# Sliding-window attention on one core: scores from 64-row products, the sink in the score tile, value differences

## The chip, the cores and the metric

The kernel runs on one core of a Trainium2 chip. Time is device time of that core in microseconds, from three timed runs; the profile is one further execution of the same program, taken by the hardware profiler. The core's engines are TensorE (PE, with its weight loads listed apart as PEld), VectorE (DVE), ScalarE (ACT), GpSimd (POOL) and SyncE (SP), which here only issues DMAs.

## The reference

One decoder layer on 2048 tokens of width 1024. A common input projection feeds two groups: a gated linear recurrence (HGRN2, 4 heads of 128) and causal sliding-window attention (8 query heads of 64 on 2 key/value heads, window 128, a learned sink logit per head). Their gated outputs go through an output projection, a residual and a layer norm. What the change touches is the attention:

```python
def swa_with_sinks(q, k, v, sinks):
    ...
    s = jnp.einsum('bnqhgd,bnkhd->bnhgqk', qb, kw).astype(jnp.float32) * (D ** -0.5)
    ...
    band = (j > t) & (j <= t + W)
    ...
    s = jnp.where(mask[None, :, None, None], s, -jnp.inf)
    ...
    m = jnp.maximum(jnp.max(s, axis=-1, keepdims=True), sink)
    p = jnp.exp(s - m)
    denom = jnp.sum(p, axis=-1, keepdims=True) + jnp.exp(sink - m)
    p = (p / denom).astype(v.dtype)
    o = jnp.einsum('bnhgqk,bnkhd->bnqhgd', p, vw)
```

and two lines of the recurrence, the forget gate and the key made of it:

```python
        f = lb + (1.0 - lb) * jax.nn.sigmoid(hf.astype(f32))
        k_in = 1.0 - f
```

## The kernel before

All matrices are float32. A projection is computed as three float32r products of a high and a low part (`wh`, `wl` of the weights, `xh`, `xl` of the input; L110 to L112, L120 to L122), 24 matmuls of 128x128 weights and 512 columns for one output tile.

The program has three stages. **Attention** (L185 to L330) goes over two key/value heads `j` and, in each, over four blocks `b` of 512 tokens. A block projects k and v (`kvp`), two tiles of q (`qp`, four query heads of 64 rows in two tiles) and two gates (`gp`). Rotary embedding works on VectorE and GpSimd (`rotate`). Then come four blocks `i` of 128 queries, in all 32 blocks (n = 0 to 15 for each `j`). **Recurrence** (L364 to L506) goes over two pairs of heads and four blocks of 512 tokens; **output** (L521 to L555) over 16 tiles of 128 tokens.

One attention block of 128 queries, before: the keys of the previous and the same 128 tokens are 256 columns. The four heads are two pairs; a pair's score tile `sp` holds two heads x 256 columns and is one bank of PSUM. q is stored as its float32r part on 64 rows and its remainder on the other 64 (L243 to L246), the keys' parts `kh` and `kl` twice, on both halves of the rows (L225 to L228), so that a product with 128 rows against `kh` and one against `kl` give a head's scores (L270, L271): 8 matmuls a block. VectorE moves the columns of the past into the masked half of the present (L275), so that one row of 128 columns holds a query's window; it takes the maximum (L276) and with the sink logit makes the shift and the sink's argument (L278 to L280). ScalarE takes the exponentials (L281 for the sink, L283 for the four heads, with their sums), VectorE adds and inverts (L291, L292), GpSimd scales the weights (L293). TensorE transposes them (`pt`, L296). The transposed weights are split into past and present: ScalarE copies them (`wtt`, L301), GpSimd masks the copy (L307), VectorE masks the original (L317), and the value products (`op`, L320) multiply each with the values of its block: 64 output rows for each pair of heads, so on half of the array's columns. The result is gated (L328) and spilled to DRAM (L329), from where the output stage reads it.

Buffers that matter: three for score tiles (`sc_ps`, L77), three for projections (`mm_ps`), one for transposes (`tr_ps`), one for value products (`o_ps`).

The program is written block after block, but a scheduler sets the order of the instructions on each engine before the kernel is built: it fits the matmuls of an attention block between those of the projections that follow. So the order on an engine is not that of the code, and the section on the change shows it at three places.

## Time and profile before

| | us |
|---|---|
| median of three runs | 951.5 |
| lowest and highest | 949.55 and 951.68 |
| profiled execution, span | 951.3 |
| TensorE busy in it | 933.0 |
| VectorE, ScalarE, GpSimd busy | 607.3, 308.4, 322.0 |

The span is that of the one profiled execution; the row of TensorE is read as the time in which at least one matmul was under way, so matmuls that overlap count once.

### The profile page before, as it was taken

The page shows a single profiled execution, that of the slowest core. Times are in us where ns is not written, and L with a number is a line of the kernel's source. Part 1 is how long each engine was busy: PE and PEld are TensorE (multiplying, and loading weights), DVE is VectorE, ACT ScalarE, POOL GpSimd, SP SyncE. Part 2 cuts the span into 40 slices and gives each one's busy share as a digit, 9 for nine tenths or more (in the row PEclk, how much of TensorE's full clock was granted, in tenths as well). Part 3 has the DMA queues.
Part 4 walks back from the last instruction along what each step waited for, and adds up shares of the span by engine and source line. Part 5 has one row for each costly group of instructions (what it writes and reads, how often), then busy time and mean ns, then how long its engine had stood idle before and what let it go on. Part 6 is the DMA issues. An engine that isn't in the chain of part 4 may idle for free.

```text
span 951.3 us, 12917 instructions
## 1 busy us (share of the span) xinstructions
PE 933.0 (98%) x4744; PEld 750.7 (79%) x4744; DVE 607.3 (64%) x1233; ACT 308.4 (32%) x785; POOL 322.0 (34%) x306
## 2 busy tenths in 40 slices
PE   8999999999998999999999999999999989999996
PEld 7878777777786777878887887888788878888885
DVE  5877887867879955726366383726458446666554
ACT  5455545544564423131142423122133211000000
POOL 1645536445447534313042642313133111111111
PEclk9999999999999999999999999999999999999998
DMA  7423243033242403002032321103013253444321
GB/s 261 165 72 123 70 158 124 33 106 106 78 151 94 127 12 101 23 12 100 1 122 78 100 100 65 47 1 102 10 56 123 78 188 134 143 152 146 113 99 57
DMA packets 33216, 91.03 MB, mean 96 GB/s; under 512 B 4224, under 2 KB 12416, under 8 KB 33152
## 3 DMA queue, kind: packets, MB, share of 16 engines
q1 hardware_dynamic: 27792, 73.41, 23.7%
q0 software_dynamic: 2912, 8.40, 2.5%
q10 hardware_dynamic: 2448, 8.39, 2.2%
q8 instruction: 37, 0.61, 0.3%
q14 instruction: 27, 0.22, 0.1%
HBM read 73.41 MB, written 16.78 MB: 95 GB/s over the span
## 4 chain that ended last, share of the span: by engine, by line
PE 85%; DVE 6%; DMA 4%; ACT 3%; issue 1%; SPq 0%; POOL 0%; POOLq 0%; DVEq 0%; ACTq 0%
PE vg L121 6%; PE vg L120 6%; PE vg L122 6%; PE po L537 6%; PE po L539 6%; PE po L538 6%; PE fp L110 3%; PE fp L111 3%; PE fp L112 3%; PE hq L112 3%; PE hq L110 3%; PE hq L111 3%; PE op L320 3%; PE qp L112 2%; PE qp L110 2%; PE qp L111 2%
## 5 line engine op out<-in xcount | busy, mean ns | idle before, releaser
L537 PE MATMUL po<-wo_h,mh 128*128 128x512 f32 (+1 forms) x264 | 103.1, 391 | 2.8 <-DVE z L540 2.8
L539 PE MATMUL po<-wo_h,ml 128*128 128x512 f32 (+1 forms) x264 | 102.0, 386 | 0.0
L538 PE MATMUL po<-wo_l,mh 128*128 128x512 f32 (+1 forms) x264 | 101.9, 386 | 0.0
L120 PE MATMUL vg<-wh_h,xh_h 128*128 128x512 f32 x256 | 100.8, 394 | 0.0
L121 PE MATMUL vg<-wh_l,xh_h 128*128 128x512 f32 x256 | 100.8, 394 | 0.0
L122 PE MATMUL vg<-wh_h,xh_l 128*128 128x512 f32 x256 | 100.7, 394 | 0.0
L98 POOL TENSOR_TENSOR xh_l<-xh_raw,xh_h 128x1024 fp32r<-128x1024 f32 x16 | 39.1, 2448 | 125.6 <-ACT xh_h L97 122.9
L540 DVE SCALAR_TENSOR_TENSOR z<-xr,po 128x512 f32<-128x512 f32 (+1 forms) x33 | 22.1, 672 | 70.3 <-PE po L539 64.3
L545 POOL TENSOR_SCALAR rs<-mv 128x1 f32<-128x1 f32 x16 | 9.4, 584 | 151.4 <-DVE mv L543 151.4
L283 ACT ACTIVATE wt<-sp,st 128x128 f32<-128x128 f32 x128 | 45.8, 365 | 44.4 <-DVE st L279 44.0
L537 PEld LDWEIGHTS po<-wo_h,mh 128*128 128x128 f32 x264 | 50.1, 190 | 12.4 <-DVE z L540 3.0
L293 POOL TENSOR_TENSOR wt<-wt,st 128x512 f32<-128x512 f32 x32 | 37.4, 1169 | 61.9 <-DVE st L292 35.2
L539 PEld LDWEIGHTS po<-wo_h,ml 128*128 128x128 f32 x264 | 50.0, 189 | 10.1
L538 PEld LDWEIGHTS po<-wo_l,mh 128*128 128x128 f32 x264 | 50.0, 189 | 9.5
L343 ACT ACTIVATE mh<-mp 128x512 fp32r<-128x512 f32 x16 | 9.6, 599 | 144.8 <-PE mp L342 144.8
L120 PEld LDWEIGHTS vg<-wh_h,xh_h 128*128 128x128 f32 x256 | 48.4, 189 | 10.1 <-issue 0.6
L121 PEld LDWEIGHTS vg<-wh_l,xh_h 128*128 128x128 f32 x256 | 48.1, 188 | 10.2 <-issue 0.6
L122 PEld LDWEIGHTS vg<-wh_h,xh_l 128*128 128x128 f32 x256 | 48.1, 188 | 9.9 <-issue 0.4
L395 DVE RECIPROCAL re<-e 128x512 f32<-128x512 f32 x16 | 53.5, 3344 | 0.0
L433 DVE SCALAR_TENSOR_TENSOR hg<-tg,vg 128x256 f32<-128x256 f32 x32 | 13.4, 420 | 60.2 <-ACT tg L431 60.2
L110 PE MATMUL fp<-xh_h,wh_h 128*128 128x512 f32 x128 | 51.2, 400 | 0.0
L110 PE MATMUL qp<-xa_h,wa_h 128*128 128x512 f32 x128 | 50.7, 396 | 0.0
(173 smaller groups left out, 2483.9 us busy)
## 6 DMA issues: line engine op xcount, KB each, us to landing
xh_raw<-in_xt_dram SPq DMA_DIRECT2D x32, 512.0 KB, 3.6
xa_raw<-in_xt_dram SPq DMA_DIRECT2D x28, 512.0 KB, 3.7
wh_raw<-in_wt_dram SPq DMA_DIRECT2D x16, 512.0 KB, 3.4
xr<-in_xn_dram SPq DMA_DIRECT2D x16, 512.0 KB, 3.6
out_dram<-y ACTq DMA_DIRECT2D x15, 512.0 KB, 2.6
wa_raw<-in_wt_dram SPq DMA_DIRECT2D x9, 512.0 KB, 4.9
cs<-in_rope_dram SPq DMA_DIRECT2D x8, 512.0 KB, 3.4
sw_spill<-mix POOLq DMA_DIRECT2D x32, 128.0 KB, 2.5
```

Source lines behind the costliest of these rows:

```text
L98: engines[lo_eng].tensor_sub(lo[:, c], raw[:, c], hi[:, c].bitcast(F32))
L110: nc.tensor.matmul(ps, lhsT=wh[:, r], rhs=xh[:, c], start=k == 0, stop=False)
L111: nc.tensor.matmul(ps, lhsT=wh[:, r], rhs=xl[:, c], start=False, stop=False)
L112: nc.tensor.matmul(ps, lhsT=wl[:, r], rhs=xh[:, c], start=False, stop=k == KT - 1)
L120: nc.tensor.matmul(ps, lhsT=xh[:, r], rhs=wh[:, c], start=k == 0, stop=False)
L121: nc.tensor.matmul(ps, lhsT=xh[:, r], rhs=wl[:, c], start=False, stop=False)
L122: nc.tensor.matmul(ps, lhsT=xl[:, r], rhs=wh[:, c], start=False, stop=k == KT - 1)
L283: nc.scalar.activation(wt_[:, s, :], sps[s // 2][:, s % 2, P:], AF.Exp, bias=st[:, 1, s : s + 1], scale=0.125, accum_out=st[:, 3, s : s + 1],)
L395: nc.vector.reciprocal(re, e[:, :, 1:129])
L537: nc.tensor.matmul(ps, lhsT=mh[:, e, :], rhs=wh[:, c], start=e == 0, stop=False)
L538: nc.tensor.matmul(ps, lhsT=mh[:, e, :], rhs=wl[:, c], start=False, stop=False)
L539: nc.tensor.matmul(ps, lhsT=ml[:, e, :], rhs=wh[:, c], start=False, stop=e == 7)
```

## The change

Scores: the q part and the q remainder of both heads of a tile now stand in two planes of full height, `q[:, 0, :]` and `q[:, 1, :]`, and a head uses the 64 rows where its q lies. A head's scores are three products on 64 rows (part x `kh`, remainder x `kh`, part x `kl`), written so that the two pairs, which lie on different halves of the rows, take turns: 12 matmuls a block. The sink's logit times 8 is copied by ScalarE into the last column of the past half, next to the 128 columns of the window, so that the exponentials run over 129 columns and their sums contain the sink. Values: instead of masking the transposed weights twice, all of them are multiplied with the previous block's values, and the masked ones of the present with the difference of the two blocks' values (`dv`), which VectorE makes once for 512 tokens. In the recurrence, `f` and `k` move to ScalarE. The store for the descriptors of GpSimd's DMAs shrinks to 4096 bytes.

```diff
@@ constants
+    nsink = const.tile([P, 8], F32, name="nsink")
+    sink8 = const.tile([P, 8], F32, name="sink8")
...
+    nc.vector.tensor_scalar(nsink, sink, -1.0, None, op0=ALU.mult)
+    nc.vector.tensor_scalar(sink8, sink, 8.0, None, op0=ALU.mult)
@@ attention, per 512 tokens
-                v = wk.tile([P, NBLK, 64], F32, tag="v", name=f"v{j}_{b}")
-                nc.scalar.activation(v, vt[:, :, 64:128], AF.Copy, scale=0.5)
+                v = wk.tile([P, NBLK + 1, 64], F32, tag="v", name=f"v{j}_{b}")
+                nc.scalar.activation(v[:, 1:, :], vt[:, :, 64:128], AF.Copy, scale=0.5)
+                dv = wk.tile([P, NBLK, 64], F32, tag="dv", name=f"dv{j}_{b}")
+                if prev_v is None:
+                    nc.vector.tensor_sub(dv[:, 1:, :], v[:, 2:, :], v[:, 1:NBLK, :])
+                else:
+                    nc.scalar.activation(v[:, 0, :], prev_v[:, NBLK, :], AF.Copy)
+                    nc.vector.tensor_sub(dv, v[:, 1:, :], v[:, 0:NBLK, :])
...
-                    nc.scalar.activation(q[0:64, 0, :], qrot[0:64], AF.Copy)
-                    nc.vector.tensor_sub(q[64:128, 0, :], qrot[0:64], q[0:64, 0, :].bitcast(F32))
-                    nc.scalar.activation(q[64:128, 1, :], qrot[64:128], AF.Copy)
-                    nc.vector.tensor_sub(q[0:64, 1, :], qrot[64:128], q[64:128, 1, :].bitcast(F32))
+                    nc.scalar.activation(q[:, 0, :], qrot, AF.Copy)
+                    nc.vector.tensor_sub(q[:, 1, :], qrot, q[:, 0, :].bitcast(F32))
@@ attention, per 128 queries
-                    for pair in range(2):
-                        sp = sc_ps(f"sp{j}_{n}_{pair}").rearrange("p (h k) -> p h k", h=2)
-                        sps.append(sp)
-                        for h in range(2):
-                            lhs = qs[h][:, pair, i * P : (i + 1) * P]
-                            kc = slice(i * P + lo, (i + 2) * P)
-                            nc.tensor.matmul(sp[:, h, lo:], lhsT=lhs, rhs=kh[:, kc], start=True, stop=False)
-                            nc.tensor.matmul(sp[:, h, lo:], lhsT=lhs, rhs=kl[:, kc], start=False, stop=True)
+                    sps = [sc_ps(f"sp{j}_{n}_{pair}").rearrange("p (h k) -> p h k", h=2) for pair in range(2)]
+                    kc = slice(i * P + lo, (i + 2) * P)
+                    for h in range(2):
+                        for step, (part, keys) in enumerate(((0, kh), (1, kh), (0, kl))):
+                            for pair in range(2):
+                                rows = slice(64 * pair, 64 * pair + 64)
+                                nc.tensor.matmul(
+                                    sps[pair][:, h, lo:],
+                                    lhsT=qs[h][rows, part, i * P : (i + 1) * P],
+                                    rhs=keys[rows, kc],
+                                    start=step == 0,
+                                    stop=step == 2,
+                                )
...
+                        s0 = 4 * j + 2 * pair
+                        nc.scalar.activation(sp[:, :, P - 1 : P], sink8[:, s0 : s0 + 2].unsqueeze(2), AF.Copy)
-                    sk = sink[:, 4 * j : 4 * j + 4]
-                    nc.vector.scalar_tensor_tensor(st[:, 1, :], st[:, 0, :], 0.125, sk, op0=ALU.mult, op1=ALU.max)
-                    nc.vector.tensor_scalar(st[:, 1, :], st[:, 1, :], -1.0, None, op0=ALU.mult)
-                    nc.vector.tensor_add(st[:, 2, :], st[:, 1, :], sk)
-                    nc.scalar.activation(st[:, 2, :], st[:, 2, :], AF.Exp)
+                    nc.vector.scalar_tensor_tensor(
+                        st[:, 1, :], st[:, 0, :], -0.125, nsink[:, 4 * j : 4 * j + 4], op0=ALU.mult, op1=ALU.min
+                    )
...
-                            sps[s // 2][:, s % 2, P:],
+                            sps[s // 2][:, s % 2, P - 1 :],
...
-                    nc.vector.tensor_add(st[:, 4, :], st[:, 2, :], st[:, 3, :])
-                    nc.vector.reciprocal(st[:, 4, :], st[:, 4, :])
-                    nc.gpsimd.tensor_mul(wt_, wt_, st[:, 4, :].unsqueeze(2).to_broadcast([P, 4, P]))
+                    nc.vector.reciprocal(st[:, 0, :], st[:, 2, :])
+                    nc.gpsimd.tensor_mul(wt_[:, :, 1:], wt_[:, :, 1:], st[:, 0, :].unsqueeze(2).to_broadcast([P, 4, P]))
...
+                    pall = wk.tile([P, 4, P], F32, tag="ptb", name=f"pall{j}_{n}", bufs=4)
+                    nc.scalar.activation(pall, pt, AF.Copy)
+                    parts = [(pall, v[:, i + (n == 0), :])]
                     if n > 0:
-                        wtt = wk.tile([P, 4, P], F32, tag="wtt", name=f"wtt{j}_{n}", bufs=1)
-                        nc.scalar.activation(wtt, pt, AF.Copy)
...
-                            nc.gpsimd.affine_select(
...
-                        else:
-                            nc.vector.tensor_mul(ptb, pt, tri_f.unsqueeze(1).to_broadcast([P, 4, P]))
-                        vv = v[:, i, :] if kb == 1 else (v[:, i - 1, :] if i > 0 else prev_v[:, NBLK - 1, :])
+                        pcur = wk.tile([P, 4, P], F32, tag="ptb", name=f"pcur{j}_{n}", bufs=4)
+                        nc.vector.tensor_mul(pcur, pt, tri_f.unsqueeze(1).to_broadcast([P, 4, P]))
+                        parts.append((pcur, dv[:, i, :]))
+                    for part, (ptb, vv) in enumerate(parts):
...
@@ recurrence
-                    nc.vector.tensor_scalar(f, th, c2[:, hd : hd + 1], c1[:, hd : hd + 1], op0=ALU.mult, op1=ALU.add)
+                    nc.scalar.activation(f, th, AF.Identity, scale=c2[:, hd : hd + 1], bias=c1[:, hd : hd + 1])
...
-                    nc.gpsimd.tensor_scalar(
...
+                    nc.scalar.activation(
+                        k.rearrange("p c t -> p (c t)"), th, AF.Identity, scale=nc2[:, hd : hd + 1], bias=c2[:, hd : hd + 1]
                     )
@@ build
-    nc = _bacc.Bacc("TRN2", target_bir_lowering=False, num_devices=1)
+    nc = _bacc.Bacc("TRN2", target_bir_lowering=False, num_devices=1, dynamic_dma_scratch_size=4096)
```

The order on TensorE at three places, before and after. A row is a line of the kernel's own file, the operation, its output and inputs (numbers behind the names tell buffers apart), and output rows x columns. First place: in the third block of 512 tokens of the first key/value head, where the q projection `qp_2_1` runs, the second pair of attention block 6 and the first pair of block 7, before:

```order
L270 MATMUL sp_6_1_919<-kh_1_674,q_1_0_720 128x256
L271 MATMUL sp_6_1_919<-kl_1_675,q_1_0_720 128x256
L270 MATMUL sp_6_1_919<-kh_1_674,q_1_1_756 128x256
L271 MATMUL sp_6_1_919<-kl_1_675,q_1_1_756 128x256
L111 MATMUL qp_2_1_1112<-xa_2_2_l,wa_2_h 128x512
L270 MATMUL sp_7_0_958<-kh_1_674,q_1_0_720 128x256
L271 MATMUL sp_7_0_958<-kl_1_675,q_1_0_720 128x256
L270 MATMUL sp_7_0_958<-kh_1_674,q_1_1_756 128x256
L271 MATMUL sp_7_0_958<-kl_1_675,q_1_1_756 128x256
```

Each pair is four products on the whole height, with one projection between the pairs. The same pairs after, with the value product of block 4 ahead of them:

```order
L321 MATMUL op_4_855<-pall_4_856,v_1_691 64x256 x2
L110 MATMUL qp_2_1_1116<-xa_2_0_h,wa_2_h 128x512
L111 MATMUL qp_2_1_1116<-xa_2_0_l,wa_2_h 128x512
L321 MATMUL op_4_855<-pcur_4_858,dv_1_693 64x256 x2
L112 MATMUL qp_2_1_1116<-xa_2_0_h,wa_2_l 128x512
L277 MATMUL sp_6_1_916<-kh_1_678,q_1_0_727 128x256 x2
L277 MATMUL sp_6_1_916<-kl_1_679,q_1_0_727 128x256
L277 MATMUL sp_6_1_916<-kh_1_678,q_1_1_761 128x256 x2
L277 MATMUL sp_6_1_916<-kl_1_679,q_1_1_761 128x256
L277 MATMUL sp_7_0_961<-kh_1_678,q_1_0_727 128x256 x2
L277 MATMUL sp_7_0_961<-kl_1_679,q_1_0_727 128x256
L309 MATMUL pt_5_896<-ident,wt_5_867 128x128 x4
```

Where four and four products stood on the whole height, six stand on the second half of the rows and then the first half's begin; three of those follow behind a transpose (`pt`). The value product's two parts stand apart. Second place: before, the value product of block 4 stood a little later, inside the transposes of block 5:

```order
L296 MATMUL pt_5_891<-ident,wt_5_864 128x128 x3
L320 MATMUL op_4_850<-ptb_4_0_853,v_0_294 64x256 x2
L320 MATMUL op_4_850<-ptb_4_1_857,v_1_687 64x256 x2
L296 MATMUL pt_5_891<-ident,wt_5_864 128x128
L111 MATMUL gp_2_0_1149<-xa_2_0_l,wa_3_h 128x512
```

Its four matmuls, one piece here, are two pieces after, with two projections between them, as the fence above shows. Third place: the end of the first attention block of a block of 512 tokens (block 4, behind the gate projection `gp_1_1`), after:

```order
L277 MATMUL sp_4_0_823<-kh_1_678,q_1_1_761 128x256
L277 MATMUL sp_4_1_824<-kh_1_678,q_1_1_761 128x256
L277 MATMUL sp_4_0_823<-kl_1_679,q_1_1_761 128x256
L277 MATMUL sp_4_1_824<-kl_1_679,q_1_1_761 128x256
L277 MATMUL sp_5_0_869<-kh_1_678,q_1_0_727 128x256 x2
L277 MATMUL sp_5_0_869<-kl_1_679,q_1_0_727 128x256
L321 MATMUL op_3_607<-pall_3_608,v_0_298 64x256 x2
L277 MATMUL sp_5_0_869<-kh_1_678,q_1_1_761 128x256 x2
L321 MATMUL op_3_607<-pcur_3_610,dv_0_300 64x256 x2
```

Here the two halves take turns in block 4, as written (eight more such rows stand ahead of these); block 5 behind it begins with its first pair alone, between the two parts of a value product.

## Rows read from the trace of the kernel before

**Rows 1.** The page's first part: engine, busy us (share of the span), instructions.

```profile
PE 933.0 (98%) x4744; PEld 750.7 (79%) x4744; DVE 607.3 (64%) x1233; ACT 308.4 (32%) x785; POOL 322.0 (34%) x306
```

**Rows 2.** The chain that ended last, its shares of the span by engine.

```profile
PE 85%; DVE 6%; DMA 4%; ACT 3%; issue 1%; SPq 0%; POOL 0%; POOLq 0%; DVEq 0%; ACTq 0%
```

**Rows 3.** Stretches (us): busy us (instructions) of PE, PEld, DVE, ACT, POOL; clock, DMA.

```profile
0.00:346.00 346.00, 338.67 (x1737) 267.02 (x1738) 276.43 (x586) 178.99 (x471) 173.39 (x157) 0.99 0.35 115
346.00:743.00 397.00, 397.00 (x2070) 320.18 (x2069) 214.52 (x447) 105.11 (x262) 119.02 (x111) 1.00 0.19 63
```

**Rows 4.** Waits of TensorE: who waited for whom, us in total, times, longest.

```profile
PE sp L270 <- ACT wt L283: 2.2, 2, 1.8
...
PE pt L296 <- POOL wt L293: 1.2, 2, 0.9
...
PE op L320 <- POOL ptb L307: 0.7, 2, 0.5
```

**Rows 5.** Timeline of TensorE: start, us, instruction, [idle before and releaser].

```profile
309.79 0.38 PE L270 MATMUL sp<-kh,q 128*128 128x256 f32 x1 [1.85 <-ACT wt L283]
...
311.43 0.63 PE L110 MATMUL fp<-xh_h,wh_h 128*128 128x512 f32 x1
311.86 0.63 PE L111 MATMUL fp<-xh_l,wh_h 128*128 128x512 f32 x1
```

**Rows 6.** The same columns as rows 3, for the stretch behind that wait.

```profile
310.50:314.00 3.50, 3.45 (x12) 2.84 (x12) 3.04 (x7) 3.50 (x6) 2.91 (x3) 0.54 0.21 80
```

**Rows 7.** Timeline: score products (L270, L271) on all rows, and one weight load.

```profile
211.37 0.28 PE L270 MATMUL sp<-kh,q 128*128 128x256 f32 x1
211.37 0.19 PEld L271 LDWEIGHTS sp<-kl,q 128*128 128x128 f32 x1
...
211.84 0.39 PE L111 MATMUL qp<-xa_l,wa_h 128*128 128x512 f32 x1
...
212.07 0.28 PE L270 MATMUL sp<-kh,q 128*128 128x256 f32 x1
```

**Rows 8.** Timeline of TensorE: value products of four and of eight instructions between full matmuls.

```profile
199.53 0.39 PE L110 MATMUL qp<-xa_h,wa_h 128*128 128x512 f32 x1
199.85 0.65 PE L320 MATMUL op<-ptb,v 128*64 128x256 f32 x4
...
200.77 0.39 PE L112 MATMUL qp<-xa_h,wa_l 128*128 128x512 f32 x1
...
220.12 0.39 PE L110 MATMUL gp<-xa_h,wa_h 128*128 128x512 f32 x1
220.43 1.08 PE L320 MATMUL op<-ptb,v 128*64 128x256 f32 x8
...
221.67 0.28 PE L271 MATMUL sp<-kl,q 128*128 128x256 f32 x1
```

**Rows 9.** Timeline of TensorE: eight L444 and eight L447 between projections of the recurrence.

```profile
356.79 0.39 PE L122 MATMUL vg<-wh_h,xh_l 128*128 128x512 f32 x1
...
357.70 0.27 PE L444 MATMUL ap<-kq 128*64 128x128 f32 x1
357.71 0.22 PE L447 MATMUL ap<-kq 128*64 128x64 f32 x1
357.81 0.38 PE L444 MATMUL ap<-kq 128*64 128x128 f32 x2
...
358.46 0.40 PE L121 MATMUL vg<-wh_l,xh_h 128*128 128x512 f32 x1
```

**Rows 10.** Groups by line and shape: busy us, mean ns of one, idle before.

```profile
L307 POOL TENSOR_SCALAR_AFFINE_SELECT ptb<-wtt 128x512 f32<-128x512 f32 x30 | 25.7, 857 | 16.1 <-ACT wtt L301 16.0
...
L386 POOL TENSOR_SCALAR k<-thf,nc,c 128x512 f32<-128x512 f32 x16 | 19.0, 1188 | 38.5 <-ACT thf L382 38.5
...
L281 ACT ACTIVATE st<-st 128x4 f32<-128x4 f32 x32 | 6.6, 207 | 0.1
```

**Rows 11.** DMA issues: queue, times, KB each, median us to landing.

```profile
sw_spill<-mix POOLq DMA_DIRECT2D x32, 128.0 KB, 2.5
```

More of the change, by code (lines that the diff above doesn't have):

```diff
@@ L260, in tile_hybrid_layer @@
                     lo = P if n == 0 else 0
-                    wt_ = wk.tile([P, 4, P], F32, tag="wt", name=f"wt{j}_{n}", bufs=2)
-                    st = wk.tile([P, 6, 4], F32, tag="st", name=f"st{j}_{n}", bufs=3)
-                    sps = []
-                    for pair in range(2):
-                        sp = sc_ps(f"sp{j}_{n}_{pair}").rearrange("p (h k) -> p h k", h=2)
-                        sps.append(sp)
-                        for h in range(2):
-                            lhs = qs[h][:, pair, i * P : (i + 1) * P]
-                            kc = slice(i * P + lo, (i + 2) * P)
-                            nc.tensor.matmul(sp[:, h, lo:], lhsT=lhs, rhs=kh[:, kc], start=True, stop=False)
-                            nc.tensor.matmul(sp[:, h, lo:], lhsT=lhs, rhs=kl[:, kc], start=False, stop=True)
+                    wt_ = wk.tile([P, 4, P + 1], F32, tag="wt", name=f"wt{j}_{n}", bufs=2)
+                    st = wk.tile([P, 3, 4], F32, tag="st", name=f"st{j}_{n}", bufs=3)
+                    sps = [sc_ps(f"sp{j}_{n}_{pair}").rearrange("p (h k) -> p h k", h=2) for pair in range(2)]
[11 more added lines that the diff above has]
+                                )
+                    for pair, sp in enumerate(sps):
                         if n == 0:
@@ L294, in tile_hybrid_layer @@
+                    nc.gpsimd.tensor_mul(wt_[:, :, 1:], wt_[:, :, 1:], st[:, 0, :].unsqueeze(2).to_broadcast([P, 4, P]))
                     pt = tr_ps(f"pt{j}_{n}")
                     for s in range(4):
-                        nc.tensor.transpose(pt[:, s, :], wt_[:, s, :], ident)
+                        nc.tensor.transpose(pt[:, s, :], wt_[:, s, 1:], ident)
                     op = o_ps(f"op{j}_{n}")
-                    halves = [1] if n == 0 else [0, 1]
+                    pall = wk.tile([P, 4, P], F32, tag="ptb", name=f"pall{j}_{n}", bufs=4)
@@ L299, in tile_hybrid_layer @@
+                    nc.scalar.activation(pall, pt, AF.Copy)
+                    parts = [(pall, v[:, i + (n == 0), :])]
                     if n > 0:
-                        wtt = wk.tile([P, 4, P], F32, tag="wtt", name=f"wtt{j}_{n}", bufs=1)
-                        nc.scalar.activation(wtt, pt, AF.Copy)
-                    for kb in halves:
-                        ptb = wk.tile([P, 4, P], F32, tag="ptb", name=f"ptb{j}_{n}_{kb}", bufs=3)
-                        if n == 0:
-                            nc.scalar.activation(ptb, pt, AF.Copy)
-                        elif kb == 0:
-                            nc.gpsimd.affine_select(
-                                ptb,
-                                wtt,
-                                pattern=[[0, 4], [-1, P]],
-                                compare_op=ALU.is_gt,
-                                fill=0.0,
-                                base=0,
-                                channel_multiplier=1,
-                            )
-                        else:
-                            nc.vector.tensor_mul(ptb, pt, tri_f.unsqueeze(1).to_broadcast([P, 4, P]))
-                        vv = v[:, i, :] if kb == 1 else (v[:, i - 1, :] if i > 0 else prev_v[:, NBLK - 1, :])
@@ L323, in tile_hybrid_layer @@
                                 rhs=ptb[:, 2 * pair : 2 * pair + 2, :],
-                                start=kb == halves[0],
-                                stop=kb == 1,
+                                start=part == 0,
+                                stop=part == len(parts) - 1,
                             )
```

3 lines of the change are left out of this document (1 added, 2 removed).

## Prediction

> **What bounds the kernel now.** I read the page first: TensorE is busy 98% of the 951.3 us span, VectorE 64%, ScalarE and GpSimd about a third [rows 1]. The reader is to see there that work taken off the other three can pay only where TensorE stands still. The chain of waits says the same: 85% of it is TensorE's own instructions, and the largest single lines are projections that this change leaves alone [rows 2]. The table by stretches then tells where TensorE stood still: 7.3 us of the first 346 us (the stage with the attention) and nothing from 346 to 743 us (the gated recurrence) [rows 3]. TensorE's own waits name the causes: in the attention stage 2.2 us for the exponentials, 1.2 us for the GpSimd product and 0.7 us for the GpSimd mask [rows 4]. So about 4 us is all that faster neighbours can give back directly. Behind the longest of these waits (1.85 us, at 309.8 us) the matmuls soon run at half speed: a projection of 512 columns, otherwise one in 0.23 us, takes 0.43 us at 311.4 us [rows 5, 7], with a granted clock of 0.54 from 310.5 to 314 us, most of it at the lower level of 1.2 GHz [rows 6]; at about half speed for 3.5 us that lost some 1.7 us more. What can be given back in this stage is thus some 6 us. Everything else must be counted in TensorE's own time.
>
> **More products.** Before, a block of 128 queries takes 8 score products on all 128 rows (the two parts of q stacked on the two halves, against kh and kl stored twice). They start 0.118 us apart, four in 0.47 us, 211.37 to 211.84 us [rows 7]. After, a block takes 12 products on 64 rows. Over 32 blocks that is 384 for 256. The time goes by the columns moved (256 take 0.118 us, the 512 of a projection 0.23 us), so I take a product on 64 rows to hold its rows as long as one on 128 does: the 128 more cost 128 x 0.118 = **15.1 us**.
>
> **Halves side by side.** No product on 64 rows stands in the trace. The nearest rows are products on 64 columns: the products L444 and L447 of the recurrence, on the two halves of the columns. The last L447 starts at 357.71 us, 0.01 us behind one L444 and ahead of the last two, from 357.81 us on, though in the program every L447 stands behind its L444 [rows 9]. So two halves of the array work at once, and one may run ahead of the other by about two instructions. I take rows for columns here. But the order of the changed kernel alternates the two halves in only 8 of 32 blocks, the first of each 512 tokens; with three score buffers the second pair of a block has to wait for a buffer, and the other 24 blocks run six products on one half and then six on the other. The 8 alternating blocks save 6 slots each, 48. Of the other blocks, 16 have a seam where a run on one half stands directly behind a run on the other; at two slots each that is 32 more. 80 x 0.118 = **-9.4 us**. The ends are 0, if halves never overlap, and, if whole runs of six pass each other at all 16 seams, (48 + 96) x 0.118 = -17.0 us.
>
> **Edges between shapes.** This is what the diff hides. The value products of a block stand as 8 instructions (two passes each) mostly in one piece. From the start of the projection before such a piece to the second matmul behind it, 220.12 to 221.67 us, are 1.55 us; less 0.23 and 0.12 for the two full matmuls leaves 1.20 us. A piece of 4 takes 199.53 to 200.77 us, 1.24 less 2 x 0.23, so 0.78 us. Four instructions more cost 0.42 us, so **each piece pays about 0.36 us** for being entered and left, whatever its length [rows 8]. Before, the order of TensorE has 93 pieces of half-array matmuls among full ones: 34 of value products and 59 of L444 with L447. After, 122: the two halves of a block's value product (pall with v, pcur with dv) are now set apart by a few projections, 60 pieces for 34, and the recurrence has 62. 29 x 0.36 = **10.4 us**, well covered by rows. On top come the score products, if 64 rows are a shape of their own: 60 pieces, some touching a value piece, so that the changes of shape rise from 186 in all to 338, or 169 pairs; less the 122 these are 47 more. 47 x 0.36 = **16.9 us**. Its ends are 0 and 16.9 us (less than nothing is excluded, since the full matmul ahead has to move its columns anyway). I take the upper, since the fixed part is there in both kinds of piece that the trace has: the piece of L444 and L447 takes 356.79 to 358.46 us, 1.67 less 2 x 0.23, of which eight L444 at 0.11 are 0.87, and 0.34 us are left [rows 9]. The Trainium skill says in TensorEngine Tiling (Array Packing), Key Properties, that a change of tiling mode drains the TensorE; for 64 columns the trace agrees with 0.36 us a piece, for 64 rows no run here shows it. By that page the 16.9 us stand, without it they fall away.
>
> **Work that lies beside TensorE.** GpSimd loses the mask, 25.7 us, and the recurrence's k, 19.0 us [rows 10]. VectorE loses three small steps a block and half the instructions of the q remainders, and gains 8 value differences. ScalarE loses every other q copy and 32 sink exponentials, and gains 64 sink copies into the score tile; at the 0.21 us of the exponential these are 13 us for 7 [rows 10]. In the recurrence it gains f and k, 32 instructions; even at the 1.19 us that GpSimd takes for a k they would be 38 us, where it is busy 105 of 397 us [rows 3, 10]. The work that hides all this is TensorE's own, full from 346 to 743 us. If that cover were gone, k would come at worst no later than now. What can be given back is the 6 us above; score buffers, on which the 1.85 us were spent, are three as before, so I take **-2 us** between 0 and -6.
>
> The new wait is the sink copy: it stands in ScalarE's queue until VectorE has moved the masked columns and TensorE has finished, and behind it stand the copies of q and of the transposed weights, for which TensorE waits before value products. Its price by rows is between nothing and the 2.2 us that TensorE now waits for the exponentials; it is inside the range. The smaller descriptor store concerns only the spills: 32 of them, one per attention block of about 10 us, land in 2.5 us [rows 11], and nobody waits for them before 743 us, so I cost it at nothing; if they queued, GpSimd's product would start up to 2.5 us late, behind several microseconds of projections.
>
> **The sum.** 15.1 - 9.4 + 10.4 + 16.9 - 2 = +31.0 us. The profiled span is 951.3 us, the median of the runs 951.5 us, so nothing has to be converted: 951.5 + 31.0 = **982.5 us**.
>
> **Rivals.** *Rows are no shape of their own.* The pieces of score products are entered and left free, the rest as above: 982.5 - 16.9 = 965.6 us. For it: among full matmuls the engine goes from 256 columns moved to 512 and back without a gap [rows 7]. Against it: the column pieces.
>
> *Halves never overlap.* The overlap in the trace is one of columns; if rows share what columns do not, -9.4 falls away: 982.5 + 9.4 = 991.9 us. For it: no row of this trace shows two 64-row products.
>
> *Weight loads come into the open.* In full matmuls the load of the next weights, 0.19 us, lies beside the running product: the load for L271 starts at 211.37 us with the product L270 [rows 7]. If on 64 rows a product behind another on the same half had to wait for its own load, then of 384 less 60 first ones and 112 changes of half, 212 would pay 0.19 us: +40 us, 1022 us. Against it speaks that row. In TensorE: Matmul & The Clock Gate, The mechanism, the Trainium skill says that loads overlap running matmuls only where the row group differs; for the full array this trace disagrees, and no run here shows it for halves.
>
> *Not slower.* One mechanism would do it: each half has a queue of its own, long enough to take a whole run, with no drain at its edges. Then 384 products take 192 slots, 64 x 0.118 = 7.5 us less than now; with 10.4 for the split value products and -2 that is 952.4 us, and with the whole 6 us given back 948. It decides only if both halves are in flight nearly everywhere and the row edges are free; the program order, with other matmuls between many runs, speaks against it.
>
> **How the numbers follow.** Forecast 0.53, free row edges 0.20, no overlap 0.15, open loads 0.05, not slower 0.05, some other wait of several microseconds 0.02. The range runs from below the free-edge case, with a little more given back, to above the case without overlap: 962 to 996 us. It leaves out open loads, the not-slower case and the tails. About 0.3%, 3 us, is what a measurement of this kernel can tell from no change. All but the not-slower case end slower by more: slower 0.95; of that case 0.03 within 0.3% and 0.02 faster.
>
> **What would show it.** In the changed profile: score products 0.118 us apart inside a run on one half, and in pairs a few ns apart where halves alternate (against it: 0.19 us more between them); some 0.36 us more, in all, around each piece of them; 60 pieces of value products; TensorE busy near 965 us at still some 98%; ScalarE busier from 346 us on without a wait of TensorE there; GpSimd about 45 us less busy. The forecast is wrong if the stretch up to the end of the attention grows by less than 10 us, or if the recurrence, which should grow by a microsecond, grows by several.

## The result and the profile after

The changed kernel takes 973.0 us (median of four runs, 971.8 to 974.3) against 951.3 us, the median of the kernel before over four runs now: a ratio of 1.0231, with a 95% interval of 1.0217 to 1.0246, or +21.7 us. It is slower, as forecast, by 70% of the forecast 31 us.

The first lines of the page of the changed kernel (span; engine, busy us and share, instructions) and its chain by engine:

```profile
span 971.4 us, 13115 instructions
...
PE 958.0 (99%) x4872; PEld 749.5 (77%) x4872; DVE 547.5 (56%) x1115; ACT 330.6 (34%) x839; POOL 267.1 (27%) x260
...
PE 90%; DMA 3%; DVE 2%; ACT 2%; POOL 1%; issue 1%; SPq 0%; POOLq 0%; DVEq 0%; ACTq 0%
```

Against [rows 1] TensorE is busy 25.0 us longer, and it stands still in 13.4 us of the span instead of 18.3. VectorE is 60 us less busy, GpSimd 55. None of that shows in the time except through the five microseconds of idle time and the half rate that follows such waits (below): the engine at 99% got more to do, the others less.

The stretches, with the columns of [rows 3] (the attention now ends near 370 us, where it ended near 346):

```profile
0.00:370.00 370.00, 366.47 (x1875) 267.55 (x1876) 228.87 (x486) 180.28 (x501) 141.15 (x128) 1.00 0.33 108
370.00:760.00 390.00, 390.00 (x2027) 314.42 (x2026) 200.23 (x423) 125.52 (x283) 97.05 (x94) 1.00 0.19 63
760.00:965.00 205.00, 201.53 (x974) 167.49 (x973) 115.85 (x204) 24.75 (x55) 27.36 (x37) 1.00 0.37 126
```

The reader is to see that TensorE stands still for 3.5 us up to 370 us, where it was 7.3 up to 346, and not at all in the recurrence. The last exponential of the attention starts at 369.4 us, before at 346.1: this stage grew by 23 us, nearly all of it work of TensorE. The first L444 of the recurrence (now L445) starts 22.6 us later than before and the last one 22.8 us later, so the recurrence itself is as long as it was. From the first output product (776.7 us, before 753.9) to the end of the span it is 194.7 us for 197.4, so 2.7 came back there.

TensorE's longest waits (who for whom, us in all, times, longest):

```profile
PE po L538 <- DVE z L541: 2.0, 1, 2.0
PE kvp L110 <- ACT xa_h L97: 1.6, 2, 1.4
PE warm L128 <- DVE wz L125: 1.1, 1, 1.1
```

The three waits of the attention stage, for the exponentials, the GpSimd product and the mask [rows 4], are gone, and so is the stretch at half rate [rows 5, 6]. The profiled execution of before had two more such stretches, one at the start and one behind the 2.8 us that TensorE waited for the first output block (columns of rows 3):

```profile
10.40:13.80 3.40, 3.14 (x7) 2.24 (x8) 2.45 (x8) 2.61 (x6) 0.00 (x0) 0.50 1.04 394
778.40:781.80 3.40, 3.40 (x9) 2.61 (x8) 3.40 (x8) 0.00 (x0) 0.82 (x2) 0.50 0.97 358
```

TensorE was busy for 10.0 us of the three stretches; at half the clock that is some 5.0 us lost. In the changed kernel the granted clock is 1.00 from 5.9 to 968.4 us. What TensorE waits for now are inputs at the start and the first output block. That last wait is put down to VectorE, but VectorE itself stood idle for 5.2 us until the load of `xr` had landed, and for 6.0 us in the kernel before.

**Where the time went.** I summed over both traces the time from each matmul's start to the next one's, by the tile written. Score products: 35.3 us before, 45.9 after. Value products 31.9 and 35.9. The projections and transposes of the attention, which the change does not touch but between which it puts the new pieces: +9.3 us (gates 4.3, queries 2.7, transposes 1.8, keys and values 0.5). The rest (output stage, recurrence, start, and the transposes of v): -3.6. Together these are +20.3, against 20.1 us between the two spans. Both sums hold the waits and the half rate, so the 9.3 and the -3.6 are net of what came back.

### The profile page after: what moved, and what is told of

It reads as the page before. It is cut to its first block, busy times and chain, and to the rows that moved or that the text cites. A ratio compares the mean times of both kernels' runs of the same rounds, so it can differ in the third digit from the quotient of the medians.

```text
span 971.4 us, 13115 instructions
## 1 busy us (share of the span) xinstructions
PE 958.0 (99%) x4872; PEld 749.5 (77%) x4872; DVE 547.5 (56%) x1115; ACT 330.6 (34%) x839; POOL 267.1 (27%) x260
## 4 chain that ended last, share of the span: by engine, by line
PE 90%; DMA 3%; DVE 2%; ACT 2%; POOL 1%; issue 1%; SPq 0%; POOLq 0%; DVEq 0%; ACTq 0%
PE vg L120 6%; PE vg L121 6%; PE vg L122 6%; PE po L538 6%; PE po L540 6%; PE po L539 6%; PE sp L277 4%; PE hq L112 3%; PE op L321 3%; PE hq L110 3%; PE hq L111 3%; PE fp L112 3%; PE qp L110 3%; PE fp L110 3%; PE fp L111 3%; PE qp L112 3%
## 5 line engine op out<-in xcount | busy, mean ns | idle before, releaser
L306 POOL TENSOR_TENSOR wt<-wt,st 128x512 f32<-128x512 f32 x32 | 33.1, 1034 | 109.6 <-DVE st L305 109.6
L120 PEld LDWEIGHTS vg<-wh_h,xh_h 128*128 128x128 f32 x256 | 48.5, 189 | 10.1 <-issue 0.4
L112 PE MATMUL gp<-xa_h,wa_l 128*128 128x512 f32 x128 | 51.7, 404 | 0.0
L111 PE MATMUL gp<-xa_l,wa_h 128*128 128x512 f32 x128 | 51.4, 402 | 0.0
L110 PE MATMUL gp<-xa_h,wa_h 128*128 128x512 f32 x128 | 51.3, 401 | 0.0
L430 ACT ACTIVATE hv<-vg 128x256 f32<-128x256 f32 x32 | 12.3, 383 | 113.5 <-PE vg L122 113.5
```

Of the source, the lines that this page charges most:

```text
L110: nc.tensor.matmul(ps, lhsT=wh[:, r], rhs=xh[:, c], start=k == 0, stop=False)
L111: nc.tensor.matmul(ps, lhsT=wh[:, r], rhs=xl[:, c], start=False, stop=False)
L112: nc.tensor.matmul(ps, lhsT=wl[:, r], rhs=xh[:, c], start=False, stop=k == KT - 1)
L120: nc.tensor.matmul(ps, lhsT=xh[:, r], rhs=wh[:, c], start=k == 0, stop=False)
```

## The experiments

A pair of changes of shape is one piece of half-array matmuls entered and left. In the program's order of TensorE there are 186 changes before and 338 after; the number is given for each kernel below. A slot is the 0.118 us that lie between the starts of two products of 256 columns; products on different halves can share one. Each ratio is to the kernel before, run on the same chip beside it; its median was 950.4 to 950.7 us.

**The scores undone.** The changed kernel with the eight products on 128 rows of before (238 changes):

```diff
-nc.scalar.activation(q[:, 0, :], qrot, AF.Copy)
-nc.vector.tensor_sub(q[:, 1, :], qrot, q[:, 0, :].bitcast(F32))
+nc.scalar.activation(q[0:64, 0, :], qrot[0:64], AF.Copy)
+nc.vector.tensor_sub(q[64:128, 0, :], qrot[0:64], q[0:64, 0, :].bitcast(F32))
...
-for step, (part, keys) in enumerate(((0, kh), (1, kh), (0, kl))):
...
+lhs = qs[h][:, pair, i * P : (i + 1) * P]
+nc.tensor.matmul(sp[:, h, lo:], lhsT=lhs, rhs=kh[:, kc], start=True, stop=False)
+nc.tensor.matmul(sp[:, h, lo:], lhsT=lhs, rhs=kl[:, kc], start=False, stop=True)
```

> The changed kernel with the score products of before (8 per block on 128 rows, q stacked as before); the sink column, the value differences and the rest stay. Theory A (each change of shape on TensorE costs about 0.17 us, 64 rows being a shape of their own): changes fall from 338 to 238, -17 us, and product slots from 288 to 256, -4 us: 952 us. Rival B (64 rows are no shape of their own): only the slots and three pieces, -5 us: 968 us. Rival C (the lost time sits in the sink copy and ScalarE's queue): it stays, 972 us.

Measured: 951.0 us, 1.0008 (0.9997 to 1.0020). Without the new scores nothing of the loss is left: the extra value pieces cost about what the shorter waits give back. TensorE's wait for the exponentials is gone here too, so that wait was removed by the rest of the change, not by the products on 64 rows.

**The scores alone.** The kernel before with the twelve products on 64 rows and the two planes of q, all else as before (268 changes).

```diff
-lhs = qs[h][:, pair, i * P : (i + 1) * P]
...
+rows = slice(64 * pair, 64 * pair + 64)
...
+lhsT=qs[h][rows, part, i * P : (i + 1) * P],
+rhs=keys[rows, kc],
```

> The kernel before with nothing but the 12 score products on 64 rows and the q planes of full height. Theory A: changes of shape 186 to 268, +14 us, slots 256 to about 290, +4 us: 969 us. Rival B: the slots alone, 955 us. Rival C: no sink copy here, so 951 us.

Measured: 965.6 us, 1.0159 (1.0140 to 1.0179), so +15.1 us. The new scores carry most of the loss by themselves.

**Full rows.** The changed kernel with its twelve products on all 128 rows, so that they are as many as after but of the shape of their neighbours (244 changes). What it leaves out stands in its expectation.

```diff
-  lhsT=qs[h][rows, part, i * P : (i + 1) * P],
-  rhs=keys[rows, kc],
+  lhsT=qs[h][:, part, i * P : (i + 1) * P],
+  rhs=keys[:, kc],
```

> The changed kernel with its 12 score products on all 128 rows instead of 64; the other head's rows are then added into each score, so this leaves out the separation of the heads and times the products alone. Theory A: changes of shape 338 to 244, -16 us, but no two halves side by side, so 384 slots for 288, +11 us: 968 us. Rival B (64 rows are no shape of their own, halves overlap): only the overlap is lost, 984 us. Rival E (halves do not overlap on 64 rows, edges cost): 957 us.

Measured: 966.6 us, 1.0167 (1.0150 to 1.0185), 6 us less than the changed kernel. The twelve products on half the rows are thus slower than the same twelve on all rows, although some of them run two at a time. TensorE in this kernel (timeline: start, us, instruction):

```profile
56.70 0.39 PE L112 MATMUL qp<-xa_h,wa_l 128*128 128x512 f32 x1
56.93 0.40 PE L277 MATMUL sp<-kh,q 128*128 128x256 f32 x2
...
58.01 0.60 PE L309 MATMUL pt<-ident,wt 128*128 128x128 f32 x4
...
59.04 0.39 PE L111 MATMUL qp<-xa_l,wa_h 128*128 128x512 f32 x1
```

and the same place in the changed kernel:

```profile
56.53 0.40 PE L112 MATMUL qp<-xa_h,wa_l 128*128 128x512 f32 x1
56.86 0.50 PE L277 MATMUL sp<-kh,q 64*128 64x256 f32 x2
57.20 0.28 PE L277 MATMUL sp<-kl,q 64*128 64x256 f32 x1
57.20 0.51 PE L277 MATMUL sp<-kh,q 64*128 64x256 f32 x4
57.54 0.29 PE L277 MATMUL sp<-kl,q 64*128 64x256 f32 x2
57.76 0.66 PE L309 MATMUL pt<-ident,wt 128*128 128x128 f32 x4
58.35 0.50 PE L277 MATMUL sp<-kh,q 64*128 64x256 f32 x2
...
59.23 0.39 PE L111 MATMUL qp<-xa_l,wa_h 128*128 128x512 f32 x1
```

Both stretches hold the same work: two projections, twelve score products (nine, then three) and four transposes between the nine and the three. On full rows they take 56.70 to 59.04 us, 2.34 us. On half rows, 56.53 to 59.23, 2.70 us: 0.36 more, although from 57.20 us on products run two at a time and three slots, 0.35 us, are saved. The two pieces pay 0.71 us for their edges, 0.36 each.

**Halves of the value product joined.** The part with the differences is put first, so that both parts, which the list scheduler had set apart, stand in one piece again (271 changes).

```diff
-parts.append((pcur, dv[:, i, :]))
+parts.insert(0, (pcur, dv[:, i, :]))
```

> The changed kernel with the two value products in the other order (differences first), so that the part that is ready later comes first and the two stay together in TensorE's order: 32 pieces instead of 60, changes of shape 338 to 271. Theory A: -67 x 0.17 = -11 us, 962 us. Rival D (the fixed part of a piece is a wait for its own operands, which splitting does not add to): 973 us, or more, since the first product now waits for VectorE.

Measured: 960.8 us, 1.0109 (1.0090 to 1.0129): 12 us less than the changed kernel for 67 changes fewer, 0.18 us each. Same instructions, same products: it is where they stand. (TensorE's waits are 1.3 us less too, 3.8 for 5.2.) The piece with the differences in the changed kernel, the other part being ahead of the first projection (timeline of TensorE):

```profile
64.47 0.49 PE L110 MATMUL gp<-xa_h,wa_h 128*128 128x512 f32 x1
64.90 0.65 PE L321 MATMUL op<-pcur,dv 128*64 128x256 f32 x4
65.48 0.49 PE L111 MATMUL gp<-xa_l,wa_h 128*128 128x512 f32 x1
```

Between the two projections lie 64.47 to 65.48 us, 1.01 less 0.23: 0.78 us, the value of [rows 8].

**Both undone.** Scores of before (the edit of the first experiment) and value products joined, the rest of the change kept (188 changes).

```diff
-parts.append((pcur, dv[:, i, :]))
+parts.insert(0, (pcur, dv[:, i, :]))
...
+lhs = qs[h][:, pair, i * P : (i + 1) * P]
```

> The changed kernel with the score products of before and the value product in one piece (differences first): 188 changes of shape, as many as before (186), and 256 slots as before. Theory A: against the run with the old scores, 50 changes fewer, -8.5 us: 942 us; what is left below the 951 us of before is what TensorE no longer waits for. Rival F (nothing is given back, the 951 us of the run with the old scores being edges against something else): 951 us.

Measured: 947.5 us, 0.9979 (0.9963 to 0.9995), between the two. What is left of the change gains 3 us and not the 8 of the theory, in part because waits that the longer kernel had covered are back: 7.4 us in all, for 5.3 with the value product split. Of TensorE's waits in it, those that are back:

```profile
PE pt L305 <- POOL wt L302: 1.5, 4, 0.7
...
PE sp L280 <- ACT wt L293: 0.6, 3, 0.3
PE ho L489 <- DVE u L469: 0.6, 1, 0.6
```

**A fourth score buffer.** It takes the accumulator bank from the projections, and lets both pairs of every block start together, so that halves alternate nearly everywhere (301 changes); and the same with the value product joined (245).

```diff
-return psp.tile([P, 512], F32, tag="mm", name=name, bufs=3)
+return psp.tile([P, 512], F32, tag="mm", name=name, bufs=2)
-return psp.tile([P, 512], F32, tag="sc", name=name, bufs=3)
+return psp.tile([P, 512], F32, tag="sc", name=name, bufs=4)
```

> The changed kernel with four score buffers and two for projections instead of three and three, so that nearly all blocks alternate the two halves. Theory A: slots from 288 to about 205, -10 us; changes of shape 338 to 301, -6 us: 957 us. Rival G (the third projection buffer hid the evacuation): TensorE waits for ScalarE and VectorE behind each of the projections and the gain is lost: 970 us or more.

> The same four score buffers with the value product in one piece: 245 changes of shape, some 205 slots. Theory A: 338 to 245, -16 us, and -10 us of slots: 947 us, below the kernel before. Rival G: 960 us or more.

Measured: 966.1 us, 1.0163 (1.0147 to 1.0178), and 961.3 us, 1.0106 (1.0082 to 1.0131): the first between the theories, the second in the range of the one on two projection buffers, though the waits are not where that theory has them, behind each of the projections. The scores did shrink, from 45.9 to 31.3 us by the same sum. An alternating block of this kernel:

```profile
210.77 0.51 PE L277 MATMUL sp<-kh,q 64*128 64x256 f32 x4
...
211.69 0.50 PE L111 MATMUL qp<-xa_l,wa_h 128*128 128x512 f32 x1
```

Its twelve products take 0.92 us until the projection starts: six slots of 0.118 us and the way out. What they gave was lost elsewhere. TensorE's waits in this kernel, and a window of its output stage (columns of rows 3):

```profile
PE po L538 <- DVE z L541: 5.0, 1, 5.0
PE mp L343 <- DVE ml L345: 2.8, 2, 1.4
```

```profile
755.00:960.00 205.00, 193.54 (x913) 159.90 (x911) 113.74 (x194) 21.28 (x43) 27.15 (x36) 0.98 0.36 123
```

Around these waits TensorE runs at half rate, too:

```profile
779.80:790.00 10.20, 5.18 (x13) 4.09 (x13) 5.43 (x9) 0.00 (x0) 1.16 (x2) 0.50 0.90 297
```

With two buffers the output products wait for VectorE to empty one, and VectorE waits for a load: in this kernel it stood 4.9 us for `xr` before the first `z`. The waits are 7.8 us, and 5.2 us busy at half the clock some 2.6 more. In the kernel with the value product joined as well, TensorE is at half rate for 15.7 busy microseconds. **The output stage on the four buffers** tests the buffers (301 changes):

```diff
-ps = mm_ps(f"po{n}_{i}")[:, : c1_ - c0]
+ps = sc_ps(f"po{n}_{i}")[:, : c1_ - c0]
```

> The changed kernel with four score buffers and two for projections, where the output stage takes its tiles from the four. If the 9 us by which the run with four score buffers fell short lie in the output stage's two buffers: 966 less 8, 958 us. Rival: they lie in the projections of the two stages ahead: 966 us.

Measured: 956.6 us, 1.0065 (1.0048 to 1.0082), as the theory of the output stage has it. The same window, 10 us earlier:

```profile
745.00:950.00 205.00, 201.03 (x971) 167.03 (x969) 117.19 (x206) 24.48 (x54) 28.44 (x38) 1.00 0.37 126
```

TensorE is busy 7.5 us more of the 205, and never at half rate. VectorE still stands before its first `z`, for 8.8 us until a DMA has landed, but with four buffers TensorE does not stand with it.

**The recurrence's f and k put back** on VectorE and GpSimd (336 changes).

```diff
-nc.scalar.activation(f, th, AF.Identity, scale=c2[:, hd : hd + 1], bias=c1[:, hd : hd + 1])
+nc.vector.tensor_scalar(f, th, c2[:, hd : hd + 1], c1[:, hd : hd + 1], op0=ALU.mult, op1=ALU.add)
-nc.scalar.activation(
-    k.rearrange("p c t -> p (c t)"), th, AF.Identity, scale=nc2[:, hd : hd + 1], bias=c2[:, hd : hd + 1]
-)
+nc.gpsimd.tensor_scalar(
+    k, th.rearrange("p (c t) -> p c t", t=P), nc2[:, hd : hd + 1], c2[:, hd : hd + 1], op0=ALU.mult, op1=ALU.add
+)
```

> The changed kernel with the recurrence's f on VectorE and k on GpSimd, as before. Theory A: 336 changes for 338, no wait of TensorE in that stage: 973 us, no difference. Rival H (moving them gave something back): 976 us or more.

Measured: 974.5 us, 1.0251 (1.0233 to 1.0270), not told apart from the changed kernel's 1.0231 (1.0217 to 1.0246). Moving 32 instructions between engines that are not the bound makes no difference here that these runs could tell.

**Changes of shape alone.** If the edges are the cause, the kernel before must gain by them too. In its recurrence a transpose on the full array stood behind each pair of half-array products. The same transposes put behind all of them (102 changes for 186) add and remove no instruction:

```diff
-nc.tensor.transpose(kp[:, 2 * i + h, :], kn[h][:, c, :], ident)
+for i in range(2):
+    for h in range(2):
+        nc.tensor.transpose(kp[:, 2 * i + h, :], kn[h][:, 2 * pr + i, :], ident)
```

> The kernel before with one move in the recurrence: the transposes (kp) stand behind all eight half-array products (ap) of a pair of chunks instead of between them. Nothing else changes, the same instructions run. It tells the price of a piece by itself: changes of shape fall from 186 to 102. Theory A: 84 changes at 0.15 us (what the runs so far give) to 0.18 us (half the 0.36 us of a piece in the trace) are 13 to 15 us: 937 us. Rival (the fixed part is a wait for operands, or the products' own length): 951 us.

Measured: 939.1 us, 0.9880 (0.9864 to 0.9897): -11.3 us for 84 changes, 0.134 us each. One place in the trace of before:

```profile
427.31 0.32 PE L444 MATMUL ap<-kq 128*64 128x128 f32 x1
427.31 0.33 PE L447 MATMUL ap<-kq 128*64 128x64 f32 x2
427.47 0.27 PE L444 MATMUL ap<-kq 128*64 128x128 f32 x1
427.67 0.33 PE L454 MATMUL kp<-ident,kq 128*128 128x128 f32 x1
427.93 0.32 PE L444 MATMUL ap<-kq 128*64 128x128 f32 x1
...
429.53 0.33 PE L454 MATMUL kp<-ident,kq 128*128 128x128 f32 x1
429.62 0.48 PE L110 MATMUL fp<-xh_h,wh_h 128*128 128x512 f32 x1
```

and the same work in the regrouped kernel:

```profile
424.78 0.32 PE L444 MATMUL ap<-kq 128*64 128x128 f32 x1
...
425.49 0.38 PE L444 MATMUL ap<-kq 128*64 128x128 f32 x2
425.80 0.66 PE L456 MATMUL kp<-ident,kq 128*128 128x128 f32 x4
426.21 0.48 PE L110 MATMUL fp<-xh_h,wh_h 128*128 128x512 f32 x1
```

Before, four groups of two L444, two L447 and a transpose take 427.31 to 429.62 us, 2.31 us. Regrouped, eight L444, eight L447 and four transposes take 424.78 to 426.21 us, 1.43: 0.88 less for six changes less, 0.147 each.

**The best of both.** The same regrouping on the kernel with old scores and joined value product (96 changes).

```diff
+parts.insert(0, (pcur, dv[:, i, :]))
...
+for i in range(2):
+    for h in range(2):
+        nc.tensor.transpose(kp[:, 2 * i + h, :], kn[h][:, 2 * pr + i, :], ident)
```

> The run with the old scores and the value product in one piece, with the same move in the recurrence: 96 changes of shape for 188. Theory A: 92 x 0.15 = 14 us below 947.5: 934 us. Rival: the gains do not add, since the value products then wait for GpSimd and ScalarE: 945 us.

Measured: 937.1 us, 0.9857 (0.9835 to 0.9880): the fastest kernel of the study, 13 us under the kernel before. It is 3 us above the theory and only 2 us under the regrouping alone, for the reason that the undone kernel showed: TensorE's waits are 11.2 us, more than the 10.1 of the kernel before. Among them:

```profile
PE ho L491 <- DVE u L471: 1.9, 2, 1.8
PE sp L280 <- ACT wt L293: 1.7, 2, 1.4
PE pt L305 <- POOL wt L302: 1.3, 3, 0.7
```

**The products on 64 rows at their best.** Four score buffers, value product joined, output stage on the four, regrouped (171 changes).

```diff
+return psp.tile([P, 512], F32, tag="sc", name=name, bufs=4)
...
+parts.insert(0, (pcur, dv[:, i, :]))
...
+        nc.tensor.transpose(kp[:, 2 * i + h, :], kn[h][:, 2 * pr + i, :], ident)
...
+ps = sc_ps(f"po{n}_{i}")[:, : c1_ - c0]
```

> Products on 64 rows at their best: four score buffers, halves alternating in nearly all blocks, value products in one piece, the recurrence's products grouped, output tiles from the four buffers. 171 changes of shape against the 96 of the same kernel with products on 128 rows. Theory A: 32 pieces of scores at some 0.35 us cost 11 us and the fewer slots give back 6 to 7; with 11 more changes elsewhere it is 5 us slower than that kernel: 939 us against 934. Rival (halves side by side pay off once they alternate): at or below 932 us.

Measured: 940.5 us, 0.9895 (0.9877 to 0.9913). Even alternating nearly everywhere, with the losses found above mended, the scores on half the rows end 3.4 us behind the scores on all rows. Up to half of that may be clock: the profiled execution has two stretches at half rate, that of the best kernel one, 1.7 us apart. Its waits are 3.3 us fewer, so they do not explain it.

## Why the prediction was right, and where its sum was off

**What bounds it** was right: the loss is TensorE's own time in the attention stage, +23 us by the trace, and neither ScalarE's extra work (125.5 us busy of 390 in the recurrence) nor GpSimd's relief shows in the time.

**The sum** is settled between the two profiled executions, 951.3 to 971.4 us: +20.1 us = 4.0 for products, 26.0 for edges, -9.9 of relief, against a forecast of 5.7, 27.3 and -2. The edges are what is left when the other two are taken from the trace. So the forecast was 11 us too high, and 8 of them lie in one term, the relief. That the time fell into the range is not what decides: the range held the case of free row edges and the one without overlap as well, and the runs tell them apart.

**More products with the overlap** (15.1 - 9.4 = +5.7 us) came to +4.0. The price per product, 0.118 us, holds. The overlap is larger: where two runs meet, three products of the next run lie beside the last of the running one (57.20 us, above), for which the prediction took two. With 16 such seams and 48 slots in the alternating blocks that makes 96; counted over the whole trace, the 384 products start in 290 slots (starts more than 0.06 us apart), which is 94 saved, 11.1 us for 9.4. The case without overlap is refuted.

**Weight loads in the open** is refuted too. Loads in the changed kernel (timeline, PEld):

```profile
56.85 0.30 PEld L277 LDWEIGHTS sp<-kh,q 64*128 64x128 f32 x2 [0.36 <-issue]
57.08 0.18 PEld L277 LDWEIGHTS sp<-kl,q 64*128 64x128 f32 x1
```

The load at 57.08 us lies beside the second product, on the same 64 rows, and its own product starts at 57.20, 0.12 us later. Loading stood still ahead of the piece, for 0.36 us, that is, at its edge. One product in a run does start late, the second, 0.22 us behind the first; it is counted with the edge here.

**Row edges** (47 x 0.36 = 16.9 us, ends 0 and 16.9) were right in kind; the rival that rows are no shape of their own is refuted, though its 965.6 us lay nearer to the result than the forecast's 982.5. The kernel on full rows has 94 slots more than the changed one, +11.1 us, and was 6.1 us faster, so the edges of the row pieces are worth 17.2 us there. The Trainium skill says in TensorEngine Tiling (Array Packing), Key Properties, that a change of tiling mode drains the TensorE; the runs agree for 64 rows as for 64 columns: a piece costs more than its products for either.

**One price for every piece** nearly held: 76 pieces at 0.36 us were to be 27.3 us, and came to 26.0, 0.34 a piece or 0.17 a change. By their medians the runs spread more: 0.134 us a change for the regrouping, 0.18 for the joining, and for the scores alone 15.1 less 4.2 for their slots in 82 changes, 0.133; and joining the value product gained 12 us beside the new scores and some 3 beside the old ones. Most of that spread is waits and half rate. Of every profiled execution, in us (waits: TensorE's in all; half rate: half of its busy time at a granted clock of 0.50):

| kernel | changes | slots | waits | half rate | span |
|---|---|---|---|---|---|
| before | 186 | 256 | 10.1 | 5.0 | 951.3 |
| after | 338 | 290 | 5.2 | 0 | 971.4 |
| scores undone | 238 | 256 | 5.3 | 0 | 949.4 |
| scores alone | 268 | 292 | 9.1 | 3.4 | 965.8 |
| full rows | 244 | 384 | 5.7 | 0 | 964.7 |
| value product joined | 271 | 294 | 3.8 | 0 | 957.9 |
| both undone | 188 | 256 | 7.4 | 0 | 944.1 |
| fourth score buffer | 301 | 204 | 13.7 | 2.6 | 964.2 |
| the same, joined | 245 | 202 | 15.6 | 7.8 | 960.6 |
| output on the four | 301 | 204 | 5.6 | 0 | 954.6 |
| f and k put back | 336 | 290 | 7.0 | 1.7 | 973.9 |
| before, regrouped | 102 | 256 | 11.6 | 1.7 | 937.2 |
| best of both | 96 | 256 | 11.2 | 1.7 | 935.8 |
| 64 rows at their best | 171 | 202 | 7.9 | 3.4 | 937.7 |

Take from each span its waits, its half rate and 0.118 us a slot: what is left lies within 2.1 us of one straight line, 876 us and 0.16 us a change. A price of its own for each kind of piece is not needed to explain these runs, and what remains of the spread, those 2 us, stays open.

**The relief** (-2 us, ends 0 and -6) is the term that was mis-sized: it came to -9.9, beyond its end. The waits of TensorE sum to 10.1 us before and 5.2 after, and the three stretches at half rate, some 5.0 us, are gone. In the attention stage that is 4.5 of waits and 1.7 of half rate: the 6 us which the prediction saw and of which it took a third, because the score buffers are three as before. The kernel with the old scores shows what failed in that reason: it has neither wait for the exponentials nor half rate [rows 4 to 6], on the same three buffers and the same score products, so the lighter work of the other engines, with the value pieces split, is enough to have buffers come free in time. Which edit of that work does it was not separated. The other 3.7 us lie at the start and in the output stage, of which the prediction says nothing: two stretches at half rate less, and 0.4 of waits. These stretches follow waits for inputs, which no edit of the change touches, so they may be the luck of one execution; and at the start the projections were only 0.5 us ahead of those before, so about 1 us of the relief, and with it of the edges, is uncertain. With both undone there are the changes and the slots of the kernel before, and the relief stands nearly alone: 7.2 us between the profiled executions, 2.7 of waits and 5.0 of half rate. With the value product joined as well, TensorE shorter again, some waits are back: part of the relief is that TensorE is slower.

**No conversion** between span and median was wrong too, though it does not move the forecast, which adds a difference to the median. Where a run has both numbers the time is some 1.7 us above the span (973.1 and 971.4 for the profiled execution after), so the profiled execution of before was one of about 953 us, 1.7 above the median of its runs. That turns the +20.1 us between the profiles into +21.7 between the medians, and of the 9.9 us of relief about 1.7 belong to that execution: its mean granted clock was 0.992, that of the others of this kernel up to 0.998.

**The sink copy** as a new wait did not come. Groups of the changed kernel (busy us, mean ns; idle before and releaser):

```profile
L385 ACT ACTIVATE f<-thf,c,c 128x512 f32<-128x512 f32 x16 | 13.1, 816 | 0.5
L387 ACT ACTIVATE k<-thf,c,nc 128x512 f32<-128x512 f32 x16 | 12.8, 801 | 0.0
L292 ACT ACTIVATE sp<-sink 128x2 f32<-128x2 f32 x64 | 10.7, 172 | 12.7 <-DVE st L290 12.6
```

ScalarE waits 12.6 us for VectorE there, as foreseen, and TensorE waits for neither. f and k take 0.8 us each against the bound of 1.19. The smaller descriptor store serves the 16 spills of the recurrence too, which the prediction left out; the attention's spills land in 2.7 us for 2.5, and TensorE waits for none.

**Not slower** was right to have little weight: its condition, both halves in flight nearly everywhere and free edges, was made true in its first half by the fourth buffer, and its second half, free edges, is what fails.

## What to carry to other kernels

When TensorE is the bound, count the changes of shape in its order before the instructions: here each cost about 0.16 us (0.13 to 0.18 by run), and moving transposes behind a run of half-array products gained 11.3 us with the same instructions. Splitting a product over two halves of the array pays only if what it saves in one piece exceeds the price of that piece: twelve products alternating take six slots for the eight of before, 0.24 us, and a piece of its own costs about 0.3 us, so it loses unless several blocks stand in one piece. Relief of the other engines is worth the waits of the bound engine and the half rate that followed them here, and no more; list both first, over the whole span. And a wait put down to an engine may be that engine's own wait for a load.

## What the hardware showed beyond that

A run on the other half does not wait for the running one to end. In the rows of the changed kernel a kl product, the third of its run of six, and a kh product both start at 57.20 us; that second one can only be the first of the other half, three products ahead of its place in the program.

Several of GpSimd's instructions that the change leaves alone got shorter, while VectorE was less busy, as with the product of the rotary embedding (groups of the kernel before, then of the changed one):

```profile
L210 POOL TENSOR_TENSOR sw_q<-sw_q,cs 128x512 f32<-128x512 f32 x16 | 23.7, 1478 | 23.5 <-DVE sw_q L209 20.4 <-DVE st L280 3.1
```

```profile
L214 POOL TENSOR_TENSOR sw_q<-sw_q,cs 128x512 f32<-128x512 f32 x16 | 22.0, 1378 | 7.0 <-DVE sw_q L213 6.9
```

GpSimd came out 55 us less busy where the removed mask and k account for 45; of the other 10, 4.3 lie in the product on the weights (1169 to 1034 ns), whose rows the change spaces 129 apart, and most of the rest in such shorter instructions. Whether the two engines share something was not tried, and the runs do not agree on it: in the kernel with the old scores, with VectorE busy 576 us for 607, the split of the inputs on GpSimd (`xa_l`) took 2969 ns for 2722.
